# Projecting one pair of query tiles ahead of attention, and two inside it

## The chip, the cores and the metric

The kernel runs on one core of a Trainium2 chip. Its time is the device time of one execution in microseconds. Before the change, three runs gave 1855.71, 1857.48 and 1858.05 us, a median of 1857.48 us. A further execution was profiled; it took 1855.84 us.

A core has several engines, each with its own queue of instructions: TensorE for matrix products (PE in the profile, with PEld for the loading of its weights), VectorE (DVE), ScalarE (ACT), GpSimd (POOL) and SyncE (SP), which starts transfers here. Each engine works through its queue in order and waits on semaphores for the others.

## The reference

A network of two layers works on 512 latent tokens and 256 context tokens of width 1024. Layer 0 mixes tokens by attention, layer 1 by a gated recurrence, and each layer ends in a convolutional feed-forward part. The change lies in the attention of layer 0, which has 16 query heads of 64 in four groups, each group with one key head and one value head:

```python
def attn_project(h, w_in, q_gain, k_gain):
    b, t, _ = h.shape
    q, k, v = jnp.split(h @ w_in, [N_HEADS * HEAD_DIM, (N_HEADS + N_KV_HEADS) * HEAD_DIM], axis=-1)
    q = rms_norm(q.reshape(b, t, N_HEADS, HEAD_DIM), q_gain)
    k = rms_norm(k.reshape(b, t, N_KV_HEADS, HEAD_DIM), k_gain)
    v = v.reshape(b, t, N_KV_HEADS, HEAD_DIM)
    return q, k, v
...
    s_win = jnp.einsum('bkgqd,bkjd->bkgqj', qb, kb).astype(jnp.float32) * scale
    s_win = jnp.where(valid, s_win, -jnp.inf)
    s_ctx = jnp.einsum('bkgqd,bkcd->bkgqc', qb, kc_t).astype(jnp.float32) * scale
    p = sink_softmax(jnp.concatenate([s_win, s_ctx], axis=-1), sink_g).astype(vb.dtype)
```

Latent queries and keys are rotated by their place on a grid after the norm. A latent query sees the latent keys of its own tile of 128 and of the tiles beside it (as far as 128 tokens away), and all context keys. Context queries see context keys alone.

## The kernel before

The 768 tokens are six tiles of 128: four latent, two of context. Tiles are projected in **pairs** (0 and 1 latent, 2 context), because one PSUM bank holds two tiles of one group's 256 query columns. A weight in float32 is held as a high part `wh` and a rest `wl`, made by ACT and DVE (lines 117 and 118), and the activations in the same way, so that a projection of one tile by `proj_tile` (line 610) is 8 x 3 = 24 matmuls, written into `pjq`.

A pair's way from there to attention is: a copy `qraw` and squares `qsq` by ACT (615, 617), their sums `qss` by DVE (619), the inverse root `qr` by POOL (441), then `qy` (632), the rotation `qt` and `qz` (640 to 648) by DVE. A result is split into parts again, `stq` for queries (722 by ACT, 723 by DVE), `sta` and `stb` for keys (704 by ACT, 705 by DVE), and PE transposes each in sets of four 128x128 blocks into `qkT` (690). ACT or DVE writes those into `qT`, `KA` or `KB` (693, 695), on which the scores work. Two banks take turns as `qkT`.

In front of the attention loop stand, in program order: `k_finish`, which does this for the keys of all three pairs, `v_finish`, and the whole projection of group 0's queries, all three pairs, by the generator `q_proj`. Then come four groups times six query tiles. For each, `attend` makes the scores `S` (lines 784 to 791) in four tiles that share two buffers, with the maximum `nm` (808, DVE), the exponential `P` (794, ACT) and the division by the sum (796, POOL). `weigh` transposes the tile before (828) and multiplies by the values (836).

The other projections are **paced work**: `others` is a generator that yields the estimated microseconds of each piece. Each of the 24 tiles adds `PER_UNIT` to what is owed, and pieces are taken until nothing is owed. Before a tile whose queries aren't projected, `attend` takes pieces until they are:

```python
while (g, qt // 2) not in ready:
    next(work)
```

Projected queries lie in `qT`, in two pools that the groups use in turn. The converted weights of one group fill four buffers each of `wh` and `wl` from `self.ws0`, the only pool that attention uses for them; one bank (`psP`) takes the paced projections in the loop. Raw weights come by SP into two buffers `wr`, which the modulation weights (`wada`, line 309) share.

The program order is not the order on the engines: a scheduler of the language orders each engine's queue by its own estimate of times, within the dependencies.

## Time and profile before

| What | Value |
|---|---|
| median of 3 runs | 1857.48 us (1855.71 to 1858.05) |
| profiled execution, its time | 1855.84 us |
| its span, first to last instruction | 1854.0 us |
| mean granted TensorE clock | 0.993 |
| DVE, ACT, POOL busy | 1213.7, 754.4, 201.6 us |
| bytes moved | 166.43 MB, 90 GB/s in the mean |

All times are from the span's start. A row of the waits says which engine and line waited for whom, with the total, the number and the longest in us. A row of the rows in order of time has its start, its length, engine, line, operation, output and inputs, sizes and count; in brackets stands the idle time of the engine before it and what ended it. A matmul's length includes its way through the array, so the starts of the next ones lie closer than its length, and overlapping ones count as busy once. The granted clock is the share of TensorE's full rate.

### The profile page before, as it was taken

The page shows a single profiled execution, that of the slowest core. Times are in us where ns is not written, and L with a number is a line of the kernel's source. Part 1 is how long each engine was busy: PE and PEld are TensorE (multiplying, and loading weights), DVE is VectorE, ACT ScalarE, POOL GpSimd, SP SyncE. Part 2 cuts the span into 40 slices and gives each one's busy share as a digit, 9 for nine tenths or more (in the row PEclk, how much of TensorE's full clock was granted, in tenths as well). Part 3 has the DMA queues.
Part 4 walks back from the last instruction along what each step waited for, and adds up shares of the span by engine and source line. Part 5 has one row for each costly group of instructions (what it writes and reads, how often), then busy time and mean ns, then how long its engine had stood idle before and what let it go on. Part 6 is the DMA issues. An engine that isn't in the chain of part 4 may idle for free.

```text
span 1854.0 us, 32305 instructions
## 1 busy us (share of the span) xinstructions
PE 1795.1 (97%) x13326; PEld 1573.2 (85%) x13326; DVE 1213.7 (65%) x2273; ACT 754.4 (41%) x1478; POOL 201.6 (11%) x203
## 2 busy tenths in 40 slices
PE   5999999998999999999999999999998999999998
PEld 4986776787888988888998888888996799899997
DVE  5576676467878686767777666677765665365462
ACT  4355555465533443433454333333332433233332
POOL 1233333101100000000001110111110000000000
PEclk9999999999999999999999999999999999999999
DMA  9204104232343433333413222121220332332321
GB/s 309 69 24 151 55 24 157 82 103 91 103 121 97 128 123 114 100 106 103 128 52 97 58 58 58 36 57 36 58 69 24 91 92 92 102 97 87 91 83 66
DMA packets 204416, 166.43 MB, mean 90 GB/s; under 512 B 5149, under 2 KB 198254, under 8 KB 199150
## 3 DMA queue, kind: packets, MB, share of 16 engines
q1 hardware_dynamic: 196608, 160.47, 28.2%
q10 hardware_dynamic: 7662, 3.92, 0.7%
q8 instruction: 104, 1.70, 0.4%
q14 instruction: 42, 0.34, 0.1%
HBM read 162.27 MB, written 2.10 MB: 89 GB/s over the span
## 4 chain that ended last, share of the span: by engine, by line
PE 89%; DVE 4%; DMA 4%; issue 1%; ACT 1%; POOL 0%; SPq 0%; ACTq 0%; POOLq 0%; DVEq 0%
PE dn L170 15%; PE pd L170 14%; PE pZ L188 8%; PE pf L170 8%; PE pV L188 4%; PE pjq L610 4%; PE pv L170 4%; PE ao L170 4%; PE ho L170 3%; PE pq L170 3%; PE pv L836 3%; PE pt L828 2%; PE pgate L170 2%; PE ada L309 2%; PE pY L188 2%; PE kv L610 2%
## 5 line engine op out<-in xcount | busy, mean ns | idle before, releaser
L117 ACT ACTIVATE wh<-wr 128x512 fp32r<-128x512 f32 (+2 forms) x328 | 194.9, 608 | 467.7 <-DMA wr<-in_ffn_w_up 76.7
L118 DVE TENSOR_TENSOR wl<-wr,wh 128x512 fp32r<-128x512 f32 (+2 forms) x328 | 218.6, 674 | 132.3 <-ACT wh L117 131.7
L170 PE MATMUL dn<-g,wh 128*128 128x512 f32 (+1 forms) x1056 | 263.2, 357 | 0.0
L170 PE MATMUL pd<-hn,wh 128*128 128x256 f32 (+1 forms) x1408 | 227.6, 284 | 1.8 <-issue 1.8
L170 PEld LDWEIGHTS dn<-g,wh 128*128 128x128 f32 x1056 | 175.3, 189 | 29.5 <-DVE g L1008 0.3
L170 PEld LDWEIGHTS pd<-hn,wh 128*128 128x128 f32 x1408 | 194.5, 190 | 3.2 <-issue 3.0
L188 PE MATMUL pZ<-hs,wh 128*128 128x386 f32 x704 | 183.0, 342 | 1.8 <-ACT t L941 1.1
L170 PE MATMUL dn<-g,wl 128*128 128x512 f32 (+1 forms) x528 | 159.3, 356 | 0.0
L140 ACT ACTIVATE wh<-wr 128x512 fp32r<-128x512 f32 x132 | 82.4, 630 | 163.7 <-PE pZ L188 35.7
L170 PE MATMUL pd<-hn,wl 128*128 128x256 f32 x704 | 141.9, 283 | 0.0
L188 PEld LDWEIGHTS pZ<-hs,wh 128*128 128x128 f32 x704 | 127.4, 189 | 12.5 <-issue 5.9
L188 PE MATMUL pZ<-hs,wl 128*128 128x386 f32 x352 | 119.0, 342 | 3.9 <-DVE wl L141 3.9
L141 DVE TENSOR_TENSOR wl<-wr,wh 128x512 fp32r<-128x512 f32 x132 | 96.1, 734 | 40.7 <-ACT wh L140 39.5
L170 PE MATMUL pf<-hn,wh 128*128 128x512 f32 (+1 forms) x512 | 118.6, 347 | 2.9 <-DVE xc L1035 1.9
L170 PEld LDWEIGHTS pd<-hn,wl 128*128 128x128 f32 x704 | 109.2, 190 | 0.0
L1035 DVE SCALAR_TENSOR_TENSOR xl<-dn,mod,xl 128x512 f32<-128x512 f32 x72 | 53.8, 747 | 72.2 <-PE dn L170 71.9
L170 PEld LDWEIGHTS dn<-g,wl 128*128 128x128 f32 x528 | 87.6, 188 | 14.8
L938 POOL TENSOR_TENSOR gg<-gg,R 128x772 f32<-128x772 f32 x22 | 45.0, 2047 | 460.1 <-DVE gg L937 447.2
L188 PE MATMUL pV<-hs,wh 128*128 128x386 f32 x352 | 92.0, 341 | 2.1 <-DVE hs L384 1.6
L170 PEld LDWEIGHTS pf<-hn,wh 128*128 128x128 f32 x512 | 80.3, 191 | 15.7 <-DVE xc L1035 2.2
L610 PE MATMUL pjq<-wh,hn 128*128 128x256 f32 x384 | 77.8, 290 | 0.0
L188 PEld LDWEIGHTS pZ<-hs,wl 128*128 128x128 f32 x352 | 66.1, 188 | 8.9 <-DVE wl L141 6.4
(302 smaller groups left out, 3762.9 us busy)
## 6 DMA issues: line engine op xcount, KB each, us to landing
wr<-in_ffn_w_up SPq DMA_DIRECT2D x88, 512.0 KB, 5.2
wada<-in_ada_w SPq DMA_DIRECT2D x40, 1024.0 KB, 4.8
wr<-in_hgrn_w_in SPq DMA_DIRECT2D x40, 512.0 KB, 4.2
ar<-in_ada_w SPq DMA_DIRECT2D x32, 256.0 KB, 7.2
wr<-in_ffn_w_down SPq DMA_DIRECT2D x8, 896.0 KB, 4.7
wr<-in_attn_w_in SPq DMA_DIRECT2D x6, 1024.0 KB, 8.3
wr<-in_ffn_w_down SPq DMA_DIRECT2D x12, 384.0 KB, 3.4
wr<-in_attn_w_out SPq DMA_DIRECT2D x8, 512.0 KB, 5.6
```

Of the source, the lines that this page charges most:

```text
L117: nc.scalar.activation(wh, src, AF.Copy)
L118: nc.vector.tensor_tensor(wl, src, f(wh), op=ALU.subtract)
L140: nc.scalar.activation(ops[i][0], src, AF.Copy)
L141: nc.vector.tensor_tensor(ops[i][1], src, f(ops[i][0]), op=ALU.subtract)
L170: nc.tensor.matmul(o, lhsT=wt, rhs=at[:, t0:t0 + o.shape[1]], start=(first and n == 0 and i == 0), stop=(last and n == len(ks) - 1 and i = ...
L188: self.nc.tensor.matmul(ps, lhsT=wt, rhs=at, start=(first and k == 0 and i == 0), stop=(k == nk - 1 and i == 2), skip_group_check=not first)
L309: nc.tensor.matmul(ps[32 * j:32 * j + 32, 0:512], lhsT=self.cs[:, k, :], rhs=raw[:, j * 512:(j + 1) * 512], start=(k == 0), stop=(k == KT ...
L610: nc.tensor.matmul(out, lhsT=x, rhs=y[:, wk], start=(start and k == 0 and j == 0), stop=(stop and k == KT - 1 and j == 2))
L828: nc.tensor.transpose(pt[:, j * P:(j + 1) * P], pr[j][:, b * P:(b + 1) * P], self.ident)
L836: nc.tensor.matmul(pv[a * HD:(a + 1) * HD, 0:256], lhsT=V[:, tl, g, :], rhs=pT[:, a * 256:(a + 1) * 256], start=(b == 0), stop=(b == len(t ...
L938: times = lambda eng, o, x, y: eng.tensor_tensor(o, x, y, op=ALU.mult)
L1035: nc.vector.scalar_tensor_tensor(x[:, d], o, self.modc(l, v, 5, d), x[:, d], op0=ALU.mult, op1=ALU.add)
```

## The change

The generator takes its weights, its `qT` tile and the list of pairs from outside; `q_open` makes the first two. In front of the loop only pair 0 of group 0 is run. The pairs 1 and 2 become the first pieces of the paced work, and what each tile adds to the owed time goes from 3.2 to 3.6.

```diff
-PER_UNIT = 3.2
+PER_UNIT = 3.6
...
-        def q_proj(psP, psT, g):
-
-            w = self.load_w([self.wcols(win, g * 256, 256)])
-            qT = qp[g % 2].tile([P, 4, TOK], F32R, tag="qT", name=f"qT{g}")
+        def q_open(g):
+
+            return self.load_w([self.wcols(win, g * 256, 256)]), qp[g % 2].tile([P, 4, TOK], F32R, tag="qT", name=f"qT{g}")
+
+        def q_proj(psP, psT, g, w, qT, pairs):
+
...
-            for pair in (0, 1, 2):
+            for pair in pairs:
...
-            stacks(z, 2)
+            stacks(z, late[2])
...
-            q0 = q_proj(psP, psT, 0)
-            for _ in q0:
+            q0 = q_open(0)
+            for _ in q_proj(psP, psT, 0, *q0, (0,)):
                 pass
...
-            yield from q_proj(psP, psT, 1)
+            yield from q_proj(psP, psT, 0, *q0, (1, 2))
+            yield from q_proj(psP, psT, 1, *q_open(1), (0, 1, 2))
             yield from ada(0, 1)
             for g in (2, 3):
-                yield from q_proj(psP, psT, g)
+                yield from q_proj(psP, psT, g, *q_open(g), (0, 1, 2))
```

Lines behind the constants move by up to three: the scores' 784 is 786 in the changed kernel, `nm`'s 808 is 810, `stq`'s 723 is 725.

The order of PE's queue just ahead of the first scores, before the change (`pjq` projection, `sta`, `stb` and `stq` the parts of keys and queries that are transposed, `S` scores):

```order
L690 MATMUL qkT<-cst,stb 128x128 x4
L610 MATMUL pjq<-wl,hn_73 128x256
L610 MATMUL pjq<-wh,hn_73 128x256 x2
L610 MATMUL pjq<-wl,hn_73 128x256
L610 MATMUL pjq<-wh,hn_73 128x256 x2
L610 MATMUL pjq<-wl,hn_73 128x256
L610 MATMUL pjq<-wh,hn_73 128x256 x2
L610 MATMUL pjq<-wl,hn_73 128x256
L610 MATMUL pjq<-wh,hn_73 128x256
L690 MATMUL qkT<-cst,stq 128x128 x4
L610 MATMUL pjq<-wh,hn_73 128x256
```

The same place after the change, from the last projection of pair 0 to the first scores:

```order
L610 MATMUL pjq<-wh,hn_73 128x256
L690 MATMUL qkT<-cst,sta 128x128 x4
L690 MATMUL qkT<-cst,stb 128x128 x4
L690 MATMUL qkT<-cst,sta 128x128 x4
L690 MATMUL qkT<-cst,stb 128x128 x4
L690 MATMUL qkT<-cst,sta 128x128 x4
L690 MATMUL qkT<-cst,stb 128x128 x4
L690 MATMUL qkT<-cst,sta 128x128 x4
L690 MATMUL qkT<-cst,stb 128x128 x4
L690 MATMUL qkT<-cst,stq 128x128 x8
L786 MATMUL S<-KA,qT_1104 128x256
```

Before, each set of four transposes has projections between it and the next; now ten sets follow each other up to the first scores. Ahead of this place the two queues are the same.

The order of DVE's queue in the same stretch, before, from the last key pair's `KB` casts to the first maximum of scores:

```order
L645 TENSOR_TENSOR qz<-qz,qt 128x256
L619 TENSOR_REDUCE qss<-qsq 128x8
L723 TENSOR_TENSOR stq<-qz,stq 128x4x64 x2
L440 TENSOR_SCALAR rv<-qss 128x8
L695 CAST KB<-qkT 128x4x128
L118 TENSOR_TENSOR wl<-wr,wh 128x512
L632 TENSOR_TENSOR qy<-qraw,qr 128x8x32 x2
L118 TENSOR_TENSOR wl<-wr,wh 128x512
L644 TENSOR_TENSOR qt<-qy,Bq 128x4x32
L118 TENSOR_TENSOR wl<-wr,wh 128x512
L640 TENSOR_TENSOR qz<-qy,Aq 128x256
```

And after the change (`rv` is what POOL makes `qr` from, for the queries of pair 0):

```order
L619 TENSOR_REDUCE qss<-qsq 128x8
L705 TENSOR_TENSOR stb<-qz,sta 128x512
L695 CAST KB<-qkT 128x4x128
L440 TENSOR_SCALAR rv<-qss 128x8
L705 TENSOR_TENSOR stb<-qz,sta 128x512
L695 CAST KB<-qkT 128x4x128
L632 TENSOR_TENSOR qy<-qraw,qr 128x8x32 x2
L695 CAST KB<-qkT 128x4x128
L644 TENSOR_TENSOR qt<-qy,Bq 128x4x32
L640 TENSOR_TENSOR qz<-qy,Aq 128x256
L644 TENSOR_TENSOR qt<-qy,Bq 128x4x32
L640 TENSOR_TENSOR qz<-qy,Aq 128x256
```

The sums and rotations of the other pairs' queries and the conversion of group 1's weights (`wl`) have left this stretch; the steps for the keys and for pair 0 remain, with two `KB` casts now ahead of `qy`.

PE's queue behind the first two score tiles, before the change; the third score tile follows at once:

```order
L784 MATMUL S<-KA,qT_1104 128x256
L785 MATMUL S<-KB,qT_1104 128x256
L791 LDWEIGHTS one_385
L791 MATMUL S<-sinkp,one_385 128x1
L784 MATMUL S<-KA,qT_1104 128x256
```

After the change, projections of pair 1 stand there, 19 matmuls up to the third score tile:

```order
L786 MATMUL S<-KA,qT_1104 128x256
L787 MATMUL S<-KB,qT_1104 128x256
L793 LDWEIGHTS one_385
L793 MATMUL S<-sinkp,one_385 128x1
L610 MATMUL pjq<-wh,hn_73 128x256
L610 MATMUL pjq<-wl,hn_73 128x256
```

What has moved in between is the paced work: pair 1 of group 0 now lies beside the first tile of the attention loop.

## The prediction

> **What bounds the kernel now.** I read the page first, then the busy time by stretches around the change, then what TensorE (PE) waits for there, then the rows of the engines in order of time. The page says which engine carries the span:

> ```profile
> span 1854.0 us, 32305 instructions
> ...
> PE 1795.1 (97%) x13326; PEld 1573.2 (85%) x13326; DVE 1213.7 (65%) x2273; ACT 754.4 (41%) x1478; POOL 201.6 (11%) x203
> ```

> PE is busy for 97% of the span, so a change of order can only win or lose PE's idle time and PE's clock. The next view is the busy time by stretches (length, then busy us and count of PE, PEld, DVE, ACT, POOL, granted clock, DMA share, GB/s):

> ```profile
> 85.20:101.90 16.70, 15.93 (x138) 15.70 (x136) 13.60 (x37) 9.91 (x19) 3.27 (x2) 1.00 0.01 1
> 101.90:106.52 4.62, 1.61 (x12) 1.35 (x12) 4.62 (x13) 1.86 (x5) 0.00 (x0) 0.84 0.28 73
> 106.52:118.00 11.48, 11.48 (x77) 10.34 (x78) 9.84 (x24) 7.21 (x18) 7.00 (x8) 0.77 0.15 64
> 118.00:320.00 202.00, 201.12 (x1568) 147.24 (x1566) 129.67 (x302) 105.97 (x261) 67.59 (x84) 1.00 0.24 84
> ```

> Up to 101.9 PE projects head 0's queries with the key transposes between them and is full. The first score matmul starts at 101.9. Then comes the only hole: 1.6 busy in 4.6 us, followed by a stretch at a reduced clock. From 118 to 320 us PE is busy for 201.1 of 202: attention is already full of paced work. The waits of PE, first from 76 to 118 us, the last row from the whole span (total, times, longest):

> ```profile
> PE S L784 <- ACT P L794: 3.0, 1, 3.0
> PE S L784 <- ACT qraw L615: 0.8, 1, 0.8
> ...
> PE ada L309 <- DMA wada<-in_ada_w: 0.9, 1, 0.9
> ```

> So the hole is two waits, 0.8 us ahead of the first scores and 3.0 us behind the first two score tiles, whose exponentials are late. What the hole does to the clock is seen in stretches of 3.4 us, PE alone (length, busy, clock, DMA share, GB/s); the last row is from elsewhere in the span:

> ```profile
> 101.60:105.00 3.40, 1.61 (x12) 1.00 0.00 0
> 105.00:108.40 3.40, 1.88 (x9) 0.50 0.88 308
> 108.40:111.80 3.40, 3.40 (x18) 0.50 0.00 0
> 440.00:442.00 2.00, 0.99 (x4) 1.00 0.00 0
> ```

> A stretch that was 47% busy (1.61 of 3.40) is followed by half clock. A stretch 55% busy does not bring it back, a full one does, at 111.8. Work at half clock runs from 106.52 to 111.8, 5.3 us, and loses half of that, 2.65 us. **Lost before, from 85.2 us on: 0.77 + 3.01 + 2.65 = 6.4 us.**

> **The change, part by part.** Nothing is added or removed: 96 projection matmuls and four sets of four transposes go from the head into attention. Their price on PE:

> ```profile
> 78.87 0.40 PE L610 MATMUL pjq<-wh,hn 128*128 128x256 f32 x2
> 79.11 0.28 PE L610 MATMUL pjq<-wl,hn 128*128 128x256 f32 x1
> 79.23 0.40 PE L610 MATMUL pjq<-wh,hn 128*128 128x256 f32 x2
> ...
> 85.09 0.40 PE L610 MATMUL pjq<-wh,hn 128*128 128x256 f32 x2
> 85.32 0.28 PE L610 MATMUL pjq<-wl,hn 128*128 128x256 f32 x1
> 85.44 0.60 PE L690 MATMUL qkT<-cst,sta 128*128 128x128 f32 x4
> 85.80 0.49 PE L610 MATMUL pjq<-wh,hn 128*128 128x256 f32 x2
> ...
> 101.90 0.38 PE L784 MATMUL S<-KA,qT 128*128 128x256 f32 x1 [0.77 <-ACT qraw L615]
> ...
> 106.52 0.58 PE L784 MATMUL S<-KA,qT 128*128 128x256 f32 x1 [3.01 <-ACT P L794]
> ...
> 107.88 1.10 PE L690 MATMUL qkT<-cst,stq 128*128 128x128 f32 x4
> ...
> 347.20 0.95 PE L170 MATMUL ao<-oh,wh 128*128 128x512 f32 x4
> ```

> Three projection matmuls start every 0.36 us (78.87 to 79.23), so 96 take 11.5 us; a set of transposes starts 0.36 us ahead of the next matmul (85.44 to 85.80), so four take 1.4 us. As PE has 0.9 us of idle time in 202 us of attention, these 12.9 us lengthen attention by as much as they shorten the head. A set of four between projections costs no more than four by themselves, so I cost the mixing at nothing. From the middle of the last head's projections on, the two orders are the same nearly row for row, so the tail and the layers behind it cost nothing. What is left is what PE does while the head is emptier.

> Up to 85.2 us (the row at 85.09 holds the first pair's last matmul) the two programs have the same order. Then, before, each step of the key chain on DVE, ACT and POOL had projections over it. Now PE has ten sets of transposes, 10 x 0.36 = 3.6 us, and waits for the chain. The chain's durations, first DVE, then POOL, then ACT:

> ```profile
> 86.85 0.68 DVE L695 CAST KB<-qkT 128x512 fp32r<-128x512 f32 x1
> 87.45 0.41 DVE L645 TENSOR_TENSOR qz<-qz,qt 128x256 f32<-128x256 f32 x1
> 87.78 0.68 DVE L619 TENSOR_REDUCE qss<-qsq 128x8 f32<-128x512 f32 x1
> 88.38 0.68 DVE L705 TENSOR_TENSOR stb<-qz,sta 128x512 fp32r<-128x512 f32 x1
> 88.97 0.16 DVE L440 TENSOR_SCALAR rv<-qss 128x8 f32<-128x8 f32 x1
> ...
> 90.72 0.69 DVE L695 CAST KB<-qkT 128x512 fp32r<-128x512 f32 x1 [1.58 <-PE qkT L690]
> ...
> 91.92 0.75 DVE L632 TENSOR_TENSOR qy<-qraw,qr 128x256 f32<-128x256 f32 x2
> 92.59 0.28 DVE L644 TENSOR_TENSOR qt<-qy,Bq 128x128 f32<-128x128 f32 x1
> ...
> 94.07 0.41 DVE L645 TENSOR_TENSOR qz<-qz,qt 128x256 f32<-128x256 f32 x1
> ...
> 95.94 0.75 DVE L723 TENSOR_TENSOR stq<-qz,stq 128x256 fp32r<-128x256 f32 x2
> ...
> 100.16 0.68 DVE L118 TENSOR_TENSOR wl<-wr,wh 128x512 fp32r<-128x512 f32 x1
> ...
> 89.28 1.64 POOL L441 TENSOR_TENSOR qr<-rv,mh 128x8 f32<-128x8 f32 x1 [5.80 <-DVE rv L440]
> ...
> 93.05 0.60 ACT L693 ACTIVATE KA<-qkT 128x512 fp32r<-128x512 f32 x1 [2.36 <-PE qkT L690]
> ...
> 95.52 0.42 ACT L722 ACTIVATE stq<-qz 128x256 fp32r<-128x256 f32 x1 [0.41 <-DVE qz L645]
> ...
> 100.73 0.63 ACT L117 ACTIVATE wh<-wr 128x512 fp32r<-128x512 f32 x1
> ```

> By the new DVE order, with these steps:
> - KB, qz, qss, stb run as before, from 86.85 to 88.97. The stb waits some 0.2 for its sta, which ACT now puts behind a KA cast. A KB cast goes ahead of rv, 0.60. So rv starts at 89.8, not 88.97.
> - POOL starts 0.31 behind rv's start and takes 1.64, so qr is there at 91.7. Meanwhile DVE does stb and KB (1.2), without the 1.58 us wait of 90.72.
> - qy takes 0.67 (91.92 to 92.59), the last KB cast 0.60: 93.0. The rotation up to the first qz takes 1.48 (92.59 to 94.07), that qz 0.41: 94.9.
> - stq on ACT 0.42, on DVE 0.4, with 0.1 between engines: 95.8. The transposes 0.60, ACT's cast of qT 0.60, some 0.1: the **first scores at 97.1 us** at full clock.
> - At half clock a set takes 1.10 in place of 0.60 (row at 107.88). Two sets lie on the chain and part of a third's delay is hidden by POOL, so up to 0.9 later: 98.0. I take 97.6, near the middle, because the clock falls somewhere inside this stretch.

> Idle time of PE from 85.2 to the first scores: 97.6 - 85.2 - 3.6 = 8.8 us (8.3 to 9.2). Behind the first scores stand 19 projection matmuls, 2.3 us, so the 3.0 us wait goes: with the second score tile they cover the reduction, the exponential and the bank's release. What is late next there would be the projection bank, of which there is one; eight transposes and two score tiles lie over ACT's 0.6 us copy of it, so nothing.

> The clock: between the last key transpose (about 92) and the first query transpose (95.8) PE has nothing, so some stretch of 3.4 us falls under the 47% of the row at 101.60. The first scores then run at half clock until a whole stretch was full, 3.4 to 6.8 us behind the start. That loses 1.7 to 3.4 us; I take the middle, 2.5.

> Two costs that the trace does not show. Head 1's weights can only be converted when the moved pairs have used head 0's (four buffers each), which now lies inside attention. A quarter costs ACT 0.63 and DVE 0.68, 1.3 us; between the last use of the first quarter and its first need stand 15 projections, two value pairs and a set, about 2.8 us, so I take nothing. Uncovered, one quarter costs 1.3 and, with the next ones behind it, about 2.5. And the 0.9 us wait for the modulation weights may go, or come as one of equal size: -0.9 to +0.9, taken as nothing, since the loads keep their distance in the order.

> **Sum:** 8.8 + 2.5 - 6.4 = **+4.9 us** (bounds 8.3 + 0 - 6.4 = +1.9 and 9.2 + 3.4 - 6.4 = +6.2). Against the profiled execution's 1855.84 us that is 1860.7. The median of the runs shown is 1.64 above that execution, so I give 1857.48 + 4.9 = **1862.4 us**.

> **The rivals.**
> 1. *The clock stays full.* Ten sets of 0.60 make half of the stretch look busy, and the row at 440 kept full clock with 0.99 of 2.00. Then +1.9: 1859.4 us. Against it: 101.60 lost the clock at 47%, and the gap ahead of the query transposes is longer. [...] Chance 0.2.
> 2. *Transposes do not hold the clock at all.* Then half clock holds from the first stretch behind 85.2, and the upper bounds meet: +6.2, 1863.7 us. [...] Chance 0.12.
> 3. *The moved work does fit into attention, and the kernel is faster.* If PE in attention only looks full (its ends are modelled; PEld has 147 of 202), the 12.9 us vanish in it. Then the first scores 4.3 us earlier, the 3.0 us wait and the 2.65 us of clock are all gained: about -10, 1847.5 us. It decides from some 5 us of hidden room on. Against it: gaps between matmuls of one kind are the same in attention as in the head. Chance 0.07.
> 4. *The weights of head 1 come late:* 2.5 us on top, 1864.9 us. Chance 0.08.
> 5. *The scheduler lifts the projections back over the head.* The built order excludes it; what is left is that several terms cancel, at about 1857.5. Chance 0.05.

> **How the numbers follow.** Forecast 0.48, the rivals as given. About 0.2% (3.7 us) is what a measurement of this kernel can tell from no change. Slower by more: the forecast less 0.06 for its lower end, rivals 2 and 4: 0.62. Within: rivals 1 and 5 and that 0.06: 0.31. Faster: 0.07. The range goes from the fastest run shown plus the lower bound without the modulation wait, 1855.71 + 1.9 - 0.9 = 1856.7, to the slowest plus the upper bound and late weights, 1858.05 + 6.2 + 2.5 = 1866.8. It leaves out rival 3.

> **What would show it.** Right: first scores between 97 and 98.5 us, PE idle for 8 to 9 us between 85 and there with DVE and ACT named as releasers, no 3 us wait behind the first two score tiles, half clock over the first scores, and the first matmul of the output projection (the row at 347.20 before) some 4 to 6 us later. Wrong: full clock from 90 to 105 us (rival 1), PE waits for wh or wl near 115 us (rival 4), or attention that grew by clearly less than 12.9 us (rival 3).

## The result, and the profile after

| | before | after |
|---|---|---|
| median (7 runs each) | 1856.73 us (1855.56 to 1858.05) | 1863.19 us (1859.17 to 1864.9) |
| ratio of the two, 95% interval | | 1.0029 (1.0019 to 1.0039) |
| profiled execution: its time, its span | 1855.84, 1854.0 us | 1863.01, 1860.9 us |
| first score matmul | 101.90 us | 97.96 us |
| first output projection `ao` | 347.20 us | 352.86 us |
| first `pZ`, the first matmul of the feed-forward part's gates | 427.48 us | 433.14 us |

The changed kernel is slower by 0.29% by the ratio; the two medians lie 6.46 us apart. The forecast was 1862.4 us in a range from 1856.7 to 1866.8. PE has the same instructions as before (13326), with 5 us more of busy time. The page's first lines:

```profile
span 1860.9 us, 32309 instructions
...
PE 1800.2 (97%) x13326; PEld 1577.5 (85%) x13326; DVE 1212.5 (65%) x2273; ACT 755.6 (41%) x1478; POOL 201.4 (11%) x203
```

More busy time for the same work can be a lower clock (three projection matmuls start every 0.64 us at half clock, as shown below, and every 0.36 at full), or matmuls that stand alone: a set of transposes counts 0.60 to 0.66 us as busy when nothing follows it closely, while between projections the next matmul starts 0.36 us behind it. The busy time by stretches (length, then busy us and count of PE, PEld, DVE, ACT, POOL, granted clock, DMA share, GB/s) shows where, and where PE is idle:

```profile
85.20:97.96 12.76, 6.56 (x42) 4.93 (x40) 10.13 (x28) 5.75 (x11) 1.94 (x1) 0.87 0.00 0
97.96:104.90 6.94, 6.94 (x33) 6.56 (x33) 2.31 (x5) 1.56 (x4) 1.38 (x2) 0.50 0.01 2
104.90:118.00 13.10, 13.10 (x107) 11.47 (x107) 7.30 (x16) 5.89 (x13) 4.85 (x5) 1.00 0.00 1
118.00:320.00 202.00, 201.99 (x1579) 150.83 (x1575) 136.27 (x320) 109.98 (x266) 67.88 (x83) 1.00 0.23 83
```

Ahead of the first scores PE is now busy for about half of 12.8 us, and idle for 6.2. Then the first 6.94 us of scores and projections run at half clock (0.50 in the rows above). From there to 320 us PE is full. What PE waits for from 76 to 118 us (the rows that the head holds; total, times, longest):

```profile
PE qkT L690 <- DVE stq L725: 4.3, 1, 4.3
PE qkT L690 <- DVE KB L695: 0.7, 2, 0.4
...
PE qkT L690 <- DVE rv L440: 0.7, 1, 0.7
...
PE qkT L690 <- ACT KA L693: 0.3, 1, 0.3
PE qkT L690 <- ACT sta L704: 0.2, 1, 0.2
```

The two waits of the scores, 3.0 and 0.8 us, are gone. In their place PE waits, 6.2 us in all, for the chain of the keys and of the first query pair, and longest ahead of the query transposes. That chain in order of time, of PE, then DVE, POOL and ACT:

```profile
85.24 0.60 PE L690 MATMUL qkT<-cst,sta 128*128 128x128 f32 x4
...
91.22 0.66 PE L690 MATMUL qkT<-cst,stb 128*128 128x128 f32 x4 [0.34 <-DVE KB L695]
96.19 1.94 PE L690 MATMUL qkT<-cst,stq 128*128 128x128 f32 x8 [4.31 <-DVE stq L725]
97.96 0.58 PE L786 MATMUL S<-KA,qT 128*128 128x256 f32 x1
...
89.62 0.16 DVE L440 TENSOR_SCALAR rv<-qss 128x8 f32<-128x8 f32 x1
...
91.90 0.76 DVE L632 TENSOR_TENSOR qy<-qraw,qr 128x256 f32<-128x256 f32 x2 [0.74 <-POOL qr L441]
92.58 0.68 DVE L695 CAST KB<-qkT 128x512 fp32r<-128x512 f32 x1
...
94.66 0.75 DVE L645 TENSOR_TENSOR qz<-qz,qt 128x256 f32<-128x256 f32 x2
95.62 0.76 DVE L725 TENSOR_TENSOR stq<-qz,stq 128x256 fp32r<-128x256 f32 x2 [0.21 <-ACT stq L724]
...
89.93 1.94 POOL L441 TENSOR_TENSOR qr<-rv,mh 128x8 f32<-128x8 f32 x1 [6.43 <-DVE rv L440]
...
97.31 0.60 ACT L693 ACTIVATE qT<-qkT 128x512 fp32r<-128x512 f32 x1 [1.42 <-PE qkT L690]
```

PE's last key transposes end at 91.88 and the first query transposes start at 96.19: the key cast, the rotation and the split of the queries lie between, on DVE (and one part of the split on ACT). The clock in stretches of one microsecond (length, PE busy, clock, DMA share, GB/s), after the stretch of 3.41 us ahead of its fall:

```profile
91.25:94.66 3.41, 0.62 (x4) 1.00 0.00 0
...
94.00:95.00 1.00, 0.00 (x0) 0.83 0.00 0
95.00:96.00 1.00, 0.00 (x0) 0.50 0.00 0
...
104.00:105.00 1.00, 1.00 (x6) 0.55 0.00 0
105.00:106.00 1.00, 1.00 (x11) 1.00 0.00 0
```

The clock falls at 94.66 and is back at 104.90, by the trace's record of it. These 10.24 us are three stretches of 3.413. The later changes in this profile lie on the same grid: 446.24, where the next half clock begins, is 100 such stretches behind 104.90, and its end at 453.06 two more. In the profile of before, 989.05 is 257 of them behind 111.83. In the last of the rows PE does 11 matmuls in a microsecond, in the one before it 6. How much a projection slows down is seen in its rows at half clock:

```profile
101.23 0.63 PE L610 MATMUL pjq<-wh,hn 128*128 128x256 f32 x2
101.65 0.41 PE L610 MATMUL pjq<-wl,hn 128*128 128x256 f32 x1
101.87 0.63 PE L610 MATMUL pjq<-wh,hn 128*128 128x256 f32 x2
```

Three matmuls start every 0.64 us here, where full clock has 0.36, so work at half clock loses 44% of its time and not a full half. The 6.94 us behind the first scores lose some 3.1 us (an estimate from these rows), and the 5.3 us of the kernel before lose 2.3.

### The profile page after: what moved, and what is told of

It reads as the page before. It is cut to its first block, busy times and chain, and to the rows that moved or that the text cites. A ratio compares the mean times of both kernels' runs of the same rounds, so it can differ in the third digit from the quotient of the medians.

```text
span 1860.9 us, 32309 instructions
## 1 busy us (share of the span) xinstructions
PE 1800.2 (97%) x13326; PEld 1577.5 (85%) x13326; DVE 1212.5 (65%) x2273; ACT 755.6 (41%) x1478; POOL 201.4 (11%) x203
## 4 chain that ended last, share of the span: by engine, by line
PE 88%; DMA 5%; DVE 4%; issue 1%; ACT 1%; SPq 0%; POOL 0%; ACTq 0%; POOLq 0%; DVEq 0%
PE dn L170 15%; PE pd L170 14%; PE pZ L188 8%; PE pf L170 8%; PE pV L188 4%; PE pjq L610 4%; PE pv L170 4%; PE ao L170 4%; DMA wr<-in_ffn_w_up 3%; PE ho L170 3%; PE pv L838 3%; PE pq L170 3%; PE pt L830 2%; PE pgate L170 2%; PE ada L309 2%; PE kv L610 2%
## 5 line engine op out<-in xcount | busy, mean ns | idle before, releaser
L117 ACT ACTIVATE wh<-wr 128x512 fp32r<-128x512 f32 (+2 forms) x328 | 194.6, 608 | 464.3 <-DMA wr<-in_ffn_w_up 76.0
L118 DVE TENSOR_TENSOR wl<-wr,wh 128x512 fp32r<-128x512 f32 (+2 forms) x328 | 219.7, 677 | 129.1 <-ACT wh L117 126.9
L170 PE MATMUL dn<-g,wh 128*128 128x512 f32 (+1 forms) x1056 | 262.8, 357 | 0.1
L170 PE MATMUL pd<-hn,wh 128*128 128x256 f32 (+1 forms) x1408 | 227.6, 284 | 1.9 <-issue 1.9
L170 PEld LDWEIGHTS dn<-g,wh 128*128 128x128 f32 x1056 | 175.2, 189 | 29.7 <-ACT g L1010 0.4
L170 PEld LDWEIGHTS pd<-hn,wh 128*128 128x128 f32 x1408 | 194.5, 190 | 3.4 <-issue 3.3
L170 PE MATMUL dn<-g,wl 128*128 128x512 f32 (+1 forms) x528 | 159.4, 356 | 0.0
L170 PE MATMUL pd<-hn,wl 128*128 128x256 f32 x704 | 141.8, 283 | 0.0
L170 PE MATMUL pf<-hn,wh 128*128 128x512 f32 (+1 forms) x512 | 117.6, 345 | 2.7 <-DVE xc L1038 1.9
L170 PEld LDWEIGHTS pd<-hn,wl 128*128 128x128 f32 x704 | 109.0, 190 | 0.0
L170 PEld LDWEIGHTS dn<-g,wl 128*128 128x128 f32 x528 | 87.7, 188 | 14.7
L170 PEld LDWEIGHTS pf<-hn,wh 128*128 128x128 f32 x512 | 79.5, 189 | 15.3 <-DVE xc L1038 2.2
L610 PE MATMUL pjq<-wh,hn 128*128 128x256 f32 x384 | 78.6, 294 | 0.0
```

The lines of the kernel that those rows point to most:

```text
L117: nc.scalar.activation(wh, src, AF.Copy)
L118: nc.vector.tensor_tensor(wl, src, f(wh), op=ALU.subtract)
L170: nc.tensor.matmul(o, lhsT=wt, rhs=at[:, t0:t0 + o.shape[1]], start=(first and n == 0 and i == 0), stop=(last and n == len(ks) - 1 and i = ...
L610: nc.tensor.matmul(out, lhsT=x, rhs=y[:, wk], start=(start and k == 0 and j == 0), stop=(stop and k == KT - 1 and j == 2))
```

## The experiments

Times come from several chips, so only a ratio to the kernel before on the same chip is compared. A local measure says more than the total: how much later the first `ao` or the first `pZ` comes than in the kernel before, each counted from the first projection of head 0 (78.55 us before), which itself shifts by some tenths, in two runs (e9, e10) by 0.8 and 1.4 us later and in e7 2.4 us sooner (there nine more matmuls stand behind it). In e9 a further half clock, from 369.38 on, lies between `ao` and `pZ`, and in e12 one of 3.41 us from 296.53 on lies inside attention.

| Kernel | ratio (95%) | first scores | half clock near the head | first `ao` | first `pZ` |
|---|---|---|---|---|---|
| before | 1 | 101.90 | 105.00, 6.83 us long | 0 | 0 |
| after | 1.0029 (1.0019 to 1.0039) | 97.96 | 94.66, 10.24 us long | +5.63 | +5.63 |
| after again (e8) | 1.0036 (1.0022 to 1.005) | 97.51 | 96.47, 3.41 | +4.07 | +4.03 |
| 24 discarded matmuls (e9) | 1.0029 (1.0019 to 1.0039) | 98.78 | 96.31, 6.83 | +4.92 | +6.74 |
| 48 discarded (e10) | 1.0003 (0.9994 to 1.0012) | 98.68 | none | +1.88 | +1.82 |
| 72 discarded (e1) | 1.0016 (1.0007 to 1.0025) | 98.68 | none | +3.28 | +3.26 |
| one pair moved (e2) | 1.0039 (1.0025 to 1.0053) | 97.36 | 102.65, 3.41 | +2.07 | +2.73 |
| before, pace 3.6 (e3) | 1.0014 (1.0004 to 1.0023) | 101.27 | 105.72, 3.41 | -0.40 | +0.24 |
| after, pace 3.2 (e4) | 1.004 (1.0028 to 1.0052) | 97.65 | 94.88, 6.83 | +5.16 | +5.14 |
| before, other pool order (e5) | 0.9985 (0.9976 to 0.9993) | 113.97 | none | +0.45 | -5.85 |
| before, paced bank first (e6) | 1.000 (0.999 to 1.001) | 103.27 | 114.46, 3.41 | -1.65 | -1.69 |
| one pair moved, other order (e7) | 1.0049 (1.0036 to 1.0062) | 114.46 | 107.12, 6.83 | +13.96 | +7.68 |
| e5 with pace 3.0 (e11) | 1.0027 (1.0015 to 1.004) | 114.00 | none | +6.70 | +0.42 |
| e5 with pace 3.4 (e12) | 0.9984 (0.9974 to 0.9995) | 115.16 | 112.21, 3.41 | +4.24 | -2.04 |

### Useless matmuls in the head's idle time

Is the cost idle time, or the clock that the idle time takes? The changed kernel, with matmuls whose results nobody reads, behind the first pair's projection:

```diff
             for _ in q_proj(psP, psT, 0, *q0, (0,)):
                 pass
+            for i in range(3):
+                ps = psP.tile([P, 512], F32, tag="pj", name="fill")
+                self.proj_tile(q0[0], hn, i, ps[:, 0:256])
```

> The changed kernel with 72 extra projection matmuls whose results are discarded, put in front of the attention, where TensorE stands idle. Theory (the loss is idle time and half clock in the emptied head): the extra work costs nothing, the clock stays full, first scores at 97.0 to 97.6 us instead of 97.96, the 3.5 us lost at half clock come back: 3.5 to 4.5 us faster than the changed kernel, 1858.5 to 1860 us. Rival (moved work is dear inside attention): as slow as the changed kernel or slower by up to 8.6 us of extra matmuls, 1863 to 1871 us.

PE's view of the stretches that were emptiest in the changed kernel (length, PE busy, clock, DMA share, GB/s):

```profile
91.25:94.66 3.41, 3.41 (x31) 1.00 0.02 5
94.66:98.00 3.34, 3.26 (x29) 1.00 0.00 0
98.00:105.00 7.00, 6.73 (x56) 1.00 0.00 0
```

The first scores come 0.7 us later than in the changed kernel, and yet the first `ao` comes 2.3 us sooner (350.56 for 352.86). 72 matmuls more, and the kernel reaches that point earlier: the work behind the first scores runs at full clock. The sizes expected were missed: the first scores come at 98.68 and not by 97.6, since 72 are more than the gap holds, and by the two ratios to before the kernel wins back 2.4 us of the changed kernel's time and not 3.5 to 4.5.

The same with `range(1)` (24 matmuls) and `range(2)` (48):

> The changed kernel with one third of the discarded matmuls of the first run (24 in place of 72, about 3.2 us), issued ahead of the query transposes; their results are thrown away. Theory: they lie in the head's idle time and add nothing to it, but they leave the last wait of the chain (4.3 us for stq) as idle as before, and the clock falls by that wait: first scores 97.5 to 98.5, a half-clock stretch of 3.4 to 10.2 us still beginning between 93 and 100, first output projection at 351 to 353.5. Rival: the clock falls by the idle time of the whole chain, so that 3.2 us less of it keep the clock full: no half clock in the head, first output projection at 349 to 350.5.

> The same with two thirds (48 discarded matmuls, about 6.4 us, standing among the first transposes). Theory: if the last wait of the chain takes the clock, it still stands (about 3 to 4 us behind the last discarded matmul) and a stretch of half clock begins between 95 and 101; first output projection at 350.5 to 353. Rival: no half clock, as with 72, and the first output projection at 349.5 to 351.

The 24 stand around the first two sets of transposes, ahead of the other eight. Most of the wait for `stq` stays, in PE's waits from 84 to 125 us:

```profile
PE qkT L690 <- DVE stq L725: 3.1, 1, 3.1
```

and the stretch ahead of the clock's fall was a quarter busy, the next two at half clock:

```profile
92.90:96.31 3.41, 0.78 (x6) 0.42 (x4) 3.33 (x11) 0.92 (x3) 0.00 (x0) 1.00 0.00 0
96.31:103.14 6.83, 6.13 (x28) 5.55 (x29) 2.91 (x6) 2.54 (x7) 0.63 (x1) 0.50 0.01 2
```

So 24 change nothing (ratio 1.0029 again): PE is idle for 3.7 us ahead of the first scores in place of 6.2, and the 3.1 us of it that lie in the last wait of the chain are enough for the clock to fall. With 48 the theory expected half clock all the same, and missed. The scheduler put them between the transposes, so that the key chain itself shifts under them, and the wait for `stq` is 0.4 us. PE's stretches:

```profile
94.66:98.00 3.34, 2.39 (x16) 1.00 0.00 0
98.00:105.00 7.00, 6.71 (x56) 1.00 0.00 0
```

The clock stays full, the ratio to before is 1.0003, and `ao` comes 1.88 us later than before. What the change costs at full clock is thus about 1.9 us. The other 2 to 4 us of it (4.07 and 5.63 in two profiles of the same kernel) are the clock. In the first of these profiles 3.75 us more are lost than with 48: 0.64 up to the first scores, where the query transposes run at half clock, and 3.11 from there to `ao`, which is the 3.1 worked out above.

### The changed kernel once more

> The changed kernel once more, on the same chip and in the same call as three kernels with other orders. Theory: the loss sits in the head's wait and the half clock behind it, and so repeats: first scores at 97.5 to 98.5, idle before them 8.5 to 9.5 us, half clock over 6 to 8 us of the first scores, first output projection at 352 to 353.5, ratio 1.002 to 1.004. Rival: the 6.9 us of the first comparison were in part chance of the later clock windows: the same head, but a ratio of 1.001 or less.

The chain repeats to a tenth (the wait for `stq` is 4.32 us), but the half clock is one stretch long instead of three:

```profile
96.08 1.59 PE L690 MATMUL qkT<-cst,stq 128*128 128x128 f32 x8 [4.32 <-DVE stq L725]
97.51 0.58 PE L786 MATMUL S<-KA,qT 128*128 128x256 f32 x1
```

```profile
93.06:96.47 3.41, 0.39 (x4) 0.42 (x5) 3.00 (x11) 0.72 (x2) 0.00 (x0) 1.00 0.00 0
96.47:99.88 3.41, 3.41 (x17) 2.89 (x16) 1.38 (x2) 0.72 (x2) 0.00 (x0) 0.50 0.02 5
```

The first row is what stood ahead of the fall, the second the stretch at half clock. Here the fall came just as the transposes began, so the very next stretch was full, and the clock was back at 99.88. In the first profile the fall came at 94.66, 1.5 us ahead of the transposes, so that stretch was not full (1.88 us of 3.41); the two behind it were (to 101.49 and to 104.90), and the clock was back only after both (I can't tell why not after one). Work at half clock from the first scores: 99.88 - 97.51 = 2.4 us, which loses 1.0 at 44%; in the first profile 6.94 us, which lose 3.1. These 2.1 us and the first scores' 0.45, less 0.8 by which a wait of the scores grew, would bring `ao` 1.7 us sooner; it came 1.66 sooner (351.20 for 352.86). By these two profiles the price of this idle time depends on where its end falls on the grid of 3.41 us; that accounts for one of the two stretches more, and the other stays open. My expectation of 6 to 8 us at half clock missed for that reason. The ratio, 1.0036, repeats the loss: the first comparison was not chance.

The grid does not stand at the same place of the span in both profiles: the chain is the same, the falls lie 1.81 us apart (94.66 and 96.47), which is no multiple of 3.41, and the lengths are three times and once 3.41.

### One pair moved instead of two

```diff
-            for _ in q_proj(psP, psT, 0, *q0, (0,)):
+            for _ in q_proj(psP, psT, 0, *q0, (0, 1)):
-            yield from q_proj(psP, psT, 0, *q0, (1, 2))
+            yield from q_proj(psP, psT, 0, *q0, (2,))
```

with the pace constant `PER_UNIT` at 3.4, between the two kernels' values.

> Half of the change: only pair 2 moves into attention, pair 1 stays in front, 3.4 owed per tile. Theory: 48 more matmuls (5.7 us) lie over the key chain, so some 4 us of idle time are left ahead of the first scores; behind them the built order has four score tiles in a row, so the wait for the exponentials comes back (2 to 3 us) with half clock (2.5). Lost 9 us against 6.4 before: 1858 to 1861 us, between the two kernels. Rival (each moved pair costs the same): 1860 us; rival (moved work is dear inside attention): 1860 us too, but with first scores at 101 us.

PE's waits from 84 to 118 us:

```profile
PE S L786 <- ACT P L796: 1.3, 2, 0.9
PE qkT L690 <- DVE KB L695: 0.8, 1, 0.8
PE qkT L690 <- DVE stq L725: 0.7, 1, 0.7
```

With one pair's matmuls over the chain the wait for `stq` falls from 4.3 to 0.7 us, but part of the wait behind the first scores is still there (1.3). At `ao` the loss is 2.07 us, some two fifths of the changed kernel's. The timed ratio, 1.0039, is larger than that explains: its runs go from 1860.62 to 1869.98 us and the profiled one, at 1860.71, is one of the two shortest. What the other runs lose, no profile here shows.

### The pace constant alone

The change raises `PER_UNIT` from 3.2 to 3.6 as well. The kernel before with 3.6, and the changed kernel with 3.2:

> The kernel before with 3.6 instead of 3.2 owed per tile, no pair moved. Theory: the head's order is unchanged, so within 1.5 us of before: 1855.5 to 1858.5 us. Rival (the pacing is what costs): 1861 to 1864 us.

> The changed kernel with 3.2 instead of 3.6 owed per tile. Theory: the head's order is that of the changed kernel, so within 1.5 us of it: 1861.5 to 1864.5 us, unless paced work left over at the end costs another 1 to 2 us. Rival (the pacing is what costs): 1857 to 1859 us.

In the kernel before, 3.6 brings `ao` 0.40 us sooner and leaves the 3.0 us wait (it stands in PE's waits as 3.4 for two, the longest 3.0); in the changed one, 3.2 brings it 0.47 us sooner and leaves the 4.3 us wait for `stq`. But the half clock was one stretch of 3.41 us shorter in both, and by the 44% that alone brings `ao` about 0.9 us sooner in the first (work at half clock from about 105.9 to 109.13 in place of 106.52 to 111.83) and 1.3 in the second (4.06 us of it in place of 6.94). So either pace, taken from the other kernel, costs about half to one microsecond at this point, within what the clock's phase makes of it, and it doesn't touch the mechanism: the waits and the half clock stay. The totals of both came out higher than that (1.0014, and 1.004 for the changed kernel's 1.0029); but with the pace of before the changed kernel loses no less, so the pace is not what costs. Both profiles have half clock at the start of the feed-forward part (0.76 in the mean from 440 to 447 in the first, from 443.04 on in the second), which the profile of before lacks (1.00 from 425 to 510).

### Other orders of the pools

The scheduler's order depends on which PSUM banks the paced projections inherit, and so on the order in which attention opens its pools. Kernel before, all three pairs in front:

```diff
-        psS = self.pool(es, "psS", 2, PSUM)
         psT = self.pool(es, "psT", 2, PSUM)
         psV = self.pool(es, "psV", 1, PSUM)
         psP = self.pool(es, "psP", 1, PSUM)
+        psS = self.pool(es, "psS", 2, PSUM)
```

> The kernel before with all six token tiles projected in front, and only the order changed in which the attention's four PSUM pools are opened (the transposes', the values' and the paced projections' first, the scores' last). TensorE's order is then 48 paced projections between the last eviction of the head's projections and the first scores, and 17 and 27 more between the first score tiles. Theory: the 3.0 us and 0.8 us waits of the first score tiles go because projections stand between them, and the half clock that followed them goes too; the first scores are later by the 48 matmuls (101.2 + 6.4 = about 107.6), and the first output projection, at 347.20 in the kernel before, comes at 341 to 344, so 3 to 6 us sooner and a time of about 1850 to 1854 where the kernel before has 1856 to 1858. Rival: the waits only move to another place of the attention, because the work paced there runs out earlier: the first output projection at 346 to 348 and the time unchanged within 0.1%.

PE's waits from 84 to 340 us, and then, in order of time, the first `pZ`:

```profile
PE qkT L690 <- DVE stq L723: 1.6, 1, 1.6
PE pjq L610 <- ACT qraw L615: 1.5, 2, 0.8
PE pv L836 <- DVE pT L833: 1.1, 1, 1.1
PE S L784 <- ACT P L794: 1.0, 2, 0.6
PE ada L309 <- DMA wada<-in_ada_w: 0.5, 1, 0.5
```

```profile
421.29 0.45 PE L188 MATMUL pZ<-hs,wh 128*128 128x386 f32 x1
```

Here 65 paced projections lie in front of the first scores (48 ahead of the last four sets of query transposes and 17 behind them, where the expectation had 48 in all), no half clock comes in the head, and attention ends 6.2 us sooner (421.29 for 427.48). `ao` is no measure here, since it is started later among other work; the expectation had named it, and so missed by that row. The time falls by less, to 0.9985 of before (3.4 us between the medians on that chip): the first `dn`, a later step of the feed-forward part, comes at 499.45, where before has 498.71, so some 7 us are given back between `pZ` and there. Half clock from 434.69 on, 6.83 us long (0.50 from 435 to 440), is part of that (some 3 us); before has full clock there:

```profile
430.00:450.00 20.00, 16.00 (x86) 1.00 0.28 90
```

and longer waits for converted weights (1.0 us for one `wh` and up to 0.4 for others, where before has 0.2 for one `wl`); PE is idle for 1.9 us more between the two marks. And 12 more matmuls into `pZ` stand ahead of that `dn`, which take 2.1 us (497.32 to 499.45): they are order, not loss. These three make about 7.

Where the 6 us up to `pZ` come from is shown in part only. PE does the same 2504 matmuls from the first projection to there in both kernels, and its idle time is nearly the same, 8.8 us for 9.0: the two waits at the first scores are gone, and the waits for `stq` and `qraw` above, 3.1 us, stand ahead of them in their place. The half clock that doesn't come is worth 2.3 us. The other 3 us no view here shows.

With `psP` alone put first, and one pair moved with the order `psT`, `psP`, `psV`, `psS`:

> The kernel before with all six tiles in front, and the pool of the paced projections opened first: 18 projections stand ahead of the first scores and 29 more before the next, then 20 scores and 8 transposes with no projection between. Theory: the 3.0 us wait goes, part of it comes back in the stretch of scores without projections; the first output projection at 343 to 346, the time 1 to 4 us under the kernel before. Rival: unchanged, first output projection at 346 to 348.

> Two pairs in front and only the third moved, with the pools opened in the order transposes, paced projections, values, scores, so that all query transposes and 18 projections stand ahead of the first scores. Theory: 6.4 us of moved matmuls lengthen the attention by what they shorten the head, the wait of about 3 us behind the first score tiles goes, and no new one comes because the statistics of the last pair are evicted under the projections: the first output projection at 343 to 347. Rival (what the changed kernel shows): the chain of the first pair's statistics ends at a time that does not depend on the order, PE stands before it, and the clock falls: first output projection at 348 to 351, slower than before by 0.1 to 0.3%.

In e6 part of the wait only moved (1.9 us of scores behind exponentials near the head). `ao` came 1.6 us sooner, as the theory had it, but the time is that of before, as the rival had it. In e7 theory and rival both missed: `ao` comes at 358.77, though as in e5 it stands later among other work, and `pZ`, at 432.77, is 5.3 us later than before. The chain of the last pair moved behind the projections that were to cover it, and PE stands ahead of its transposes longer than in any other run:

```profile
108.14 1.97 PE L690 MATMUL qkT<-cst,stq 128*128 128x128 f32 x8 [4.90 <-DVE stq L725]
```

Last, e5 with the pace at 3.0 and at 3.4:

> The kernel before with the pools' order of e5_tfirst and the pace constant at 3.0 in place of 3.2, so that the paced work lasts longer. Theory: the 2 to 3 us that the attention of e5_tfirst waits in its last third (1.1, 0.8, 0.5 us behind transposes and evictions, once the paced projections have run out at 271.7) become less: first match of the feed-forward stage (421.29 in e5_tfirst) at 418.5 to 420.5, time 0 to 3 us under e5_tfirst. Rival: that wait does not hang on the projections: 421 to 422.5, the time the same within 0.1%.

> The pools' order of e5_tfirst with the pace constant at 3.4 (3.2 there, 3.0 in e11_tf30, which came 6.3 us later to the first match of the feed-forward stage, with 3.7 us of waits of scores on exponentials). Theory: denser projections take more of such waits, so the first match of the feed-forward stage comes at 419 to 421 (421.29 at 3.2) and the time lies 0 to 2 us under that of e5_tfirst. Rival: 3.2 was a lucky fit and the projections now run out sooner than the work that waits beside them: 422 to 428, and a ratio to the kernel before of 1.000 to 1.003.

At 3.0 the theory missed: `pZ` comes at 427.60, 6.3 us later than at 3.2, and the scores wait for exponentials more often (in PE's waits from 118 to 421 us, in e5 1.0):

```profile
PE S L784 <- ACT P L794: 3.7, 6, 1.4
```

Not all of the 6.3 us is in those waits, and where the rest goes stays open. At 3.4 it comes at 424.99, where the rival had it, and yet the time is 0.9984 of before, that of e5 within the intervals. e5 and e12 beat the kernel before and the changed one, by 0.15% against before; nothing better was found.

## Why the prediction was right, step by step

1. **The mechanism held, and the likeliest case with it.** Of the signs named for it these came: first scores at 97.96 (97 to 98.5), DVE and ACT as releasers of the idle time ahead of them, no wait behind the first two score tiles, half clock over the first scores, `ao` 5.66 us later (4 to 6). The 8 to 9 us of idle time are not in the trace as such: PE's waits there make 6.2 us. They are a count, with each set of transposes taken at the 0.36 us that it costs between projections.
2. **The idle time, 8.8 us, comes by the same count to 97.96 - 85.24 - 3.6 = 9.1.** The chain ran as worked out: `rv` at 89.62 (89.8), `qy` at 91.90 (91.7), the last key cast at 92.58, `qz` from 94.66. POOL's step took 1.94 us in place of 1.64, of which the earlier `rv` gave back 0.2. The query transposes started at 96.19 in place of 95.8, and from there to the first scores it took 1.8 us in place of 1.3, since they ran at half clock, as the upper bound of 98.0 had it.
3. **The clock term was the one mis-sized: 2.5 us taken, some 3.1 found**, inside its bounds of 1.7 and 3.4. Two errors in it lie against each other. The working let the clock be back after 3.4 to 6.8 us behind the first scores, and it was 6.94; and it took work at half clock to lose half, where the rows show 44%. The second profile had 1.0, below the lower bound, because there the fall landed on the transposes and the half clock ended during the scores. The term hangs on the phase of the clock's grid, so the middle of its range was a guess at a mean, and that one profile lies near the far end is chance.
4. **The moved work, 12.9 us on both sides.** From the first scores to the first `ao` it is 254.9 us now and 245.3 before, +9.6. Terms: 12.9, less the 3.0 us wait, less the 0.9 us wait for modulation weights, plus 0.8 of clock (3.1 for 2.3) and 0.3 of scores, make 10.1, so the moved work weighed some 0.5 us less than 12.9. In the head it did so too: before, 16.7 us from 85.2 to the first scores less 0.77 of wait and 3.6 of key and first-pair transposes leave 12.3. It cancels, as the sum had assumed. Attention did not take the work in for nothing (rival 3 out), and no cost of mixing it shows.
5. **The waits.** No wait for `wh` or `wl` stands between 118 and 320 us, so the weights of head 1 were hidden (rival 4 out). The wait for modulation weights went, which was the lower of the bounds given (-0.9). In the later half of attention a wait of scores grew by 0.3:

```profile
PE S L786 <- ACT P L796: 1.1, 1, 1.1
PE pt L830 <- POOL Pc L798: 0.4, 1, 0.4
```

6. **The sum.** What before lost is 0.77 + 3.01 + 2.3 = 6.1 us by the 44%, not 6.4. With these terms 9.1 + 3.1 - 6.1 - 0.9 + 0.3 = +5.5, and `ao` shows +5.66, for +4.9 forecast. That the total came so near is in part luck: the 0.6 too little of clock and 0.3 of idle time are met by the 0.9 of a wait that the sum had left at nothing. The medians differ by 6.46, the profiles' spans by 6.9; of the latter, 1.2 us come after attention. Half clock stood at the start of the feed-forward part in the profile of after,

```profile
446.24:453.06 6.82, 6.24 (x17) 5.01 (x16) 4.78 (x9) 1.65 (x3) 2.81 (x1) 0.50 0.45 154
```

where before had none (the row of 430 to 450 above; its first half clock behind attention comes at 989). No run ties it to the change: of the 14 profiles only before, e1 and e10 are without it, so two that have the change lack it (1.00 in each stretch from 425 to 510 in e1), and e3, e5 and e6, which have all pairs in front, have it (0.76 in the mean from 440 to 447 in e3, 0.50 from 435 to 440 in e5). The kernel before was profiled once. The prediction had nothing behind attention, so it could not have this.

7. **Rivals 1 and 2.** From 85.24 to 91.88 PE had transposes alone, and the clock stayed full until 94.66. On the clock's grid a stretch with nothing but transposes, 87.84 to 91.25, was busy for 2.21 us of 3.41 and kept full clock, and so did two such stretches in e8 (1.97 and 1.75). So rival 2 is out: its condition, half clock from the first stretch on, did not occur. Rival 1, full clock and +1.9, did not occur in the changed kernel either, but e10 made it: +1.88 at `ao` and a ratio of 1.0003. The chances given to the two, 0.2 and 0.12, were my estimates.

## What to carry to other kernels

Work that covers a dependent chain on other engines is not free to move, even when it is only put off: taking 12.9 us of projections away left 9 us of PE's time without use by the count above (6.2 us as waits), and the engine that bounds the kernel got back only what it had waited elsewhere (3.8 us). When such an engine is left idle, count its clock as well: it was half to two thirds of the loss here, and 48 useless matmuls in the gap brought the time back to that of before. Where a wait's cover stands counts as well: in e5 paced projections among the query transposes and ahead of the first scores removed the two waits of the scores and the half clock. Waits of 3.1 us came ahead of the first scores in place of these, though, so what that order is shown to gain is the clock; attention ended 6 us sooner, about half of it from a source that no view shows, and the whole kernel gained 0.15%.
